# Returning half of a split weight unit early, with shorter split lead and one fewer reserved unit, in a two-layer decoder kernel

## The chip, the cores and the metric

The kernel runs on one core of a Trainium2 chip. The metric is the device time of one execution in microseconds (us), from repeated runs; the profile is of one further execution. Engines are named as in the profile: PE (TensorE matmul) and PEld (its weight load), DVE (VectorE), ACT (ScalarE), POOL (GpSimd), SP (SyncE, which issues nearly all DMAs). A "q" behind a name (SPq, DVEq, PEldq) means the engine's sequencer: branches, waits and DMA issues that don't count as busy.

## The reference, cut to what matters

Two post-norm layers over 256 positions of width 1024. Each has a mixer (chunked gMLP and gated linear attention) and an FFN: dense SwiGLU in layer 0, a top-2-of-8 mixture of SwiGLU experts in layer 1. The mixture is where the time goes:

```python
def swiglu(x, w_gate, w_up, w_down):
    return (jax.nn.silu(x @ w_gate) * (x @ w_up)) @ w_down

def moe_swiglu(x, w_router, e_gate, e_up, e_down):
    ...
    for e in range(N_EXPERTS):
        out = out + gates[:, e:e + 1] * swiglu(t, e_gate[e], e_up[e], e_down[e])
    return out.reshape(B, S, D)
```

The expert width is 3584, so each of the eight experts has three matrices of 1024 x 3584 float32, 14 MB each. All of them are read once from HBM. Of the 256 positions about a quarter go to each expert.

## The kernel before, in words

**Slots and units.** All weights pass through one pool of slots of 128 x 2048 float32 (1 MB each): 16, and 18 once the second mixer has closed. A unit is 1 MB of a weight matrix. `Stream.load` (line 163) takes a slot, `r`, and issues the unit's DMA on SP (L169). `converting` (line 176) takes two more slots, `h` and `l`, and splits the unit into two rounded halves (`split`, line 262: ACT copies `r` to `h` in L263, DVE writes `l = r - h` in L264); then `r` is given back. A unit marked `whole` (the first of each gate product) isn't split: it stays in `r` and PE reads it as plain float32 (L1042). The list `idle` holds free slots: slots are taken from its front and given back at its end, in the order in which the program is written. The wait for the slot's last reader is put on the engine that writes it next.

**Who sets the order.** The program is emitted by hand. A "tick" is one k-step of a product: one tick per 512-column matmul group of a unit, four per unit. At each tick `pump` (line 198) decides what is emitted:

```python
while self.loaded < len(self.plan) and (
        len(idle) > 1 + max(0, self.freed + self.reserve - self.split)):
    self.load()
if not most or self.split >= min(self.cap, len(self.plan)) or len(idle) < 2:
    break
if self.plan[self.split][4] > self.now + lead:
    break
self.convert()
```

So units are split when they are due within `lead` ticks (`LEAD_E = 14` in the mixture, line 36), and loads leave enough idle slots for `reserve` split units that PE hasn't finished with (`NC = 6`, line 34); both are set at line 1185. `free` (line 218) gives back all slots of a unit, and is called for two units at once, behind the second one (L1055 in `product`, L1137 in `down`).

**Experts.** Each expert has four groups of hidden columns, 512, 1024, 1024, 1024 wide (the last expert in reverse order). A group is a gate product, an up product (`product`, line 1027), and then the down product (`down`, line 1112) of the group before, so that the activation (`gated`, `finish`, `transposed`) lies beside matmuls. Before its first group an expert gathers its positions with a one-hot matmul (`gather`, line 1000: `oh` on DVE, L971 to L978, transposed and multiplied on PE, L1004 and L992, then split on ACT and DVE, L983 and L984); after its last group it scatters its result (`scatter`, line 1141: `yh` and `yl` by ACT and DVE, L1154 and L1155 on PE, L1157 on DVE).

**Two ways by a bit.** An expert with at most 64 positions packs the high and low halves of its input side by side, so that a matmul by `h` and one by `l` do the work of three passes; one with more takes three passes. `cases` (line 956) chooses on the chip, with `tc.If(self.wide > 0)` (L961), on PE, ACT and DVE. `wide` is the expression `mask & 2 ** e` (line 900) over a loaded register. In this data six experts take the first way and two (the first and the third) the second. Within a product the second unit's last matmul and the passes that only the three-pass way has stand inside the branch, behind both units (`last_passes`, line 1020); a first unit's `l` is read by matmuls outside the branch alone.

**The end.** `gb` (the last norm's weights) takes a slot at line 1229. A branch for the case that an expert has more than 128 positions follows (L1237, not taken here; its body takes and returns slots of its own while it is emitted). Behind it `y` and `sq` take a slot each (lines 1283 and 1284), and the last norm writes them (`centre`, L1291 on ACT, L1293 on DVE).

Of the kernel before, what the change touches and what calls it, by code (L numbers as in the profile page):

```python
# [8 lines left out]
F32 = mybir.dt.float32  # L9
# [8 lines left out]
D = 1024  # L18
# [12 lines left out]
NX = 2  # L31
NR = 6
NQ = 3
NC = 6
HALF = 64
LEAD_E = 14


@with_exitstack
def trunk(ctx: ExitStack, tc: tile.TileContext, x, w_in, gm_ws, gm_bs, gm_ln_g, gm_ln_b, gla_wa2, gla_ba,  # L40
          gla_norm_g, w_out, ln_mix_g, ln_mix_b, ffn_g, ffn_u, ffn_d, router_w, exp_g, exp_u, exp_d,
          ln_ffn_g, ln_ffn_b, out):
    nc = tc.nc
# [14 lines left out]
    def s2(name, dt=F32, shape=(P, 512)):  # L58
        return act.tile(list(shape), dt, tag="s2", name=name, bufs=6)
# [64 lines left out]
    idle = list(range(NS))  # L124
    room = [wt] * NS

    class Stream:
# [84 lines left out]
        def get(self, key):  # L212
            i = self.index[key]
            while self.split <= i:
                self.convert()
            return self.parts[i]

        def free(self, key):
            assert self.index[key] == self.freed, (key, self.index[key], self.freed)
# [4 lines left out]
    W = Stream()  # L224
# [594 lines left out]
    def moe(xT, ready, consts):  # L819
# [38 lines left out]
        def routing():  # L858
            yield 2
            logits(0)  # L860
            yield 8
            ready.finish()
            logits(1)
            yield 2
            for tb in range(2):
                nc.tensor.matmul(plt[:, tb, :], lTs[tb], pair, start=True, stop=True)
            nc.vector.tensor_copy(lg, plt)
            m1, oh1 = first_max(lg, "1")
            lg2 = const.tile([P, 2, NE], F32, name="lg2")
            nc.vector.scalar_tensor_tensor(lg2, oh1, -3.0e38, lg, op0=ALU.mult, op1=ALU.add)  # L870
            m2, oh2 = first_max(lg2, "2")
            nc.vector.tensor_tensor(sel, oh1, oh2, op=ALU.add)
            W.pump(1, 100)
            ut = s2("ut")[:, 0:P]
            nc.gpsimd.memset(ut, 1.0)
            nc.gpsimd.affine_select(ut, ut, pattern=[[1, P]], compare_op=ALU.is_ge, fill=0.0, base=-1,
                                    channel_multiplier=-1)
            yield 6

            pr = psy("pr", (P, 2, NE))  # L880
            nc.tensor.matmul(pr[:, 0, :], ut, sel[:, 0, :], start=True, stop=True)
            nc.tensor.matmul(pr[:, 1, :], ut, sel[:, 1, :], start=True, stop=False)
            nc.tensor.matmul(pr[:, 1, :], ones, sel[:, 0, :], start=False, stop=True)
            pc = psy("pc", (P, NE))
            for tb in range(2):
                nc.tensor.matmul(pc, ones, sel[:, tb, :], start=tb == 0, stop=tb == 1)
            nc.vector.scalar_tensor_tensor(rk, pr, 1.0, sel, op0=ALU.add, op1=ALU.mult)
            nc.vector.tensor_scalar(rk, rk, -1.0, None, op0=ALU.add)
            nc.vector.tensor_scalar(small, pc, HALF + 0.5, float(-HALF), op0=ALU.is_lt, op1=ALU.mult)

            bits = const.tile([P, NE], F32, name="bits")
            msum = const.tile([P, 1], F32, name="msum")
            nc.vector.scalar_tensor_tensor(bits, pc, HALF + 0.5, powers, op0=ALU.is_gt, op1=ALU.mult)
            nc.vector.tensor_reduce(msum, bits, axis=AX.X, op=ALU.add)
            nc.vector.tensor_copy(mask_i, msum)
            experts[0].one_hot()
            mask = nc.values_load(mask_i[0:1, 0:1], engines=[ET.PE, ET.Activation, ET.DVE], min_val=0,
                                  max_val=2 ** NE - 1)
            for e in range(NE):
                experts[e].wide = mask & 2 ** e  # L900
            W.pump(1, 100)
            yield 1
            yield from experts[0].gather()

            cnt = const.tile([P, 1], F32, name="cnt")
            nc.vector.tensor_reduce(cnt, pc, axis=AX.X, op=ALU.max)
            nc.vector.tensor_copy(cnt_i, cnt)
            W.hold = False
            yield 60

            w12 = const.tile([P, 2, 2], F32, name="w12")
            dl = const.tile([P, 2], F32, name="dl")
            nc.vector.tensor_tensor(dl, m2[:, :, 0], m1[:, :, 0], op=ALU.subtract)
            nc.gpsimd.tensor_tensor(dl, ecst, dl, op=ALU.pow)
            nc.vector.tensor_scalar(w12[:, 0, :], dl, 1.0, None, op0=ALU.add)
            nc.vector.reciprocal(w12[:, 0, :], w12[:, 0, :])
            nc.vector.tensor_tensor(w12[:, 1, :], dl, w12[:, 0, :], op=ALU.mult)
            for tb in range(2):
                nc.vector.tensor_scalar(gates[:, tb, :], oh1[:, tb, :], w12[:, 0, tb:tb + 1], None, op0=ALU.mult)
                nc.vector.scalar_tensor_tensor(gates[:, tb, :], oh2[:, tb, :], w12[:, 1, tb:tb + 1], gates[:, tb, :],  # L920
                                               op0=ALU.mult, op1=ALU.add)
                nc.vector.tensor_scalar(acc[tb], xf[tb], ALPHA, None, op0=ALU.mult)
# [20 lines left out]
        class Expert:  # L943
# [83 lines left out]
            def product(self, units, n, nm):  # L1027

                xh, xl = self.x
                nb = n // 512  # L1030
                p = [psw(f"{nm}{b}") for b in range(nb)]
                kk = 2048 // n
                held, rest, last = [], [], []
                for u, ((wh, wl), free) in enumerate(units):
                    held.append(free)
                    for j in range(kk):
                        k = kk * u + j
                        for b in range(nb):
                            s = slice(b * 512, b * 512 + 512)
                            tick()  # L1040
                            if wl is None:
                                nc.tensor.matmul(p[b], self.xw[:, k, :], wh[:, j, s], start=k == 0, stop=False,  # L1042
                                                 skip_group_check=True)
                                continue
                            nc.tensor.matmul(p[b], xh[:, k, :], wh[:, j, s], start=k == 0, stop=False,  # L1045
                                             skip_group_check=True)
                            rest.append((p[b], xl[:, k, :], wh[:, j, s], False))
                            second = p[b], xh[:, k, :], wl[:, j, s], k == KT - 1
                            if k == KT - 1 or (u % 2, j, b) == (1, kk - 1, nb - 1):
                                last.append(second)  # L1050
                            else:
                                nc.tensor.matmul(*second[0:3], start=False, stop=False, skip_group_check=True)  # L1052
                    if u % 2 and (nb > 1 or u == 1):
                        self.last_passes(rest, last)
                        for free in held:  # L1055
                            free()
                        held, rest, last = [], [], []
                return p
# [53 lines left out]
            def down(self, g, units, first, final):  # L1112
                if first:
                    self.y = ybanks
                held, rest, last = [], ([], []), []
                for u, ((wh, wl), free) in enumerate(units):
                    held.append(free)
                    ch, cl = self.hT[g][u // 2]
                    ending = final and u == 2 * len(self.hT[g]) - 1
                    for n in range(4):  # L1120
# [3 lines left out]
                        y = self.y[hf]  # L1124
# [8 lines left out]
                        else:  # L1133
                            nc.tensor.matmul(y, ch[:, k, :], wl[:, j, s], start=False, stop=False,  # L1134
                                             skip_group_check=True)
                    if u % 2:
                        for free in held:  # L1137
                            free()
                        held, rest = [], ([], [])
# [20 lines left out]

        def stream(keys):
            for key in keys:
                yield W.get(key), lambda key=key: W.free(key)

        experts = [Expert(str(e), lambda tb, e=e: rk[:, tb, e:e + 1], lambda tb, e=e: gates[:, tb, e:e + 1],
                          small[:, e:e + 1]) for e in range(NE)]
# [16 lines left out]
        while W.hold:  # L1183
            tasks["route"].step()
        W.lead, W.reserve = LEAD_E, NC
        for i, t in enumerate((ybanks, ybanks, tbanks, tbanks)):
# [16 lines left out]
        for e, ex in enumerate(experts):  # L1203
            for g, (c0, n) in enumerate(groups(e)):
# [21 lines left out]
                hidden_tasks[e, g] = task  # L1226
                if g == NG - 2 and e + 1 < NE:
                    tasks["gather", e + 1] = Task(experts[e + 1].gather_from_scratch())
        gb, _ = W.slot("gb", F32, 2, D)
        for i, v in enumerate((ln_ffn_g[1], ln_ffn_b[1])):  # L1230
            nc.sync.dma_start(gb[:, i, :], bcast(v, D))
        hidden_tasks[prev].finish()
# [4 lines left out]
        with tc.If(most > P):  # L1237
# [4 lines left out]
            with tc.For_i(0, NE) as ei:  # L1242
# [14 lines left out]
                def units(plan):  # L1257

                    own = Stream()
                    plan(own)  # L1260
                    for key in list(own.index):
                        yield own.get(key), lambda key=key: own.free(key)

                def cols_of(t, g):
                    return units(lambda o: o.cols((), w(t), g * 512, 512))
# [14 lines left out]
                                        op=ALU.add)  # L1280


        y, _ = W.slot("y", F32, 2, D)
        sq, _ = W.slot("sq", F32, 2, D)
        mean, var, ssq = tiny("mean", 2), tiny("var", 2), tiny("ssq", 4).rearrange("p (t h) -> p t h", t=2)
        nc.vector.tensor_tensor(mean, total[:, :, 0], total[:, :, 1], op=ALU.add)
        nc.vector.tensor_scalar(mean, mean, -1.0 / D, None, op0=ALU.mult)
# [103 lines left out]
```

## Time and profile before

| | |
|---|---|
| three runs | 1353.36, 1355.66, 1359.66 us (median 1355.66) |
| profiled execution, own time | 1355.74 us |
| its span, first to last instruction | 1354.0 us |
| mean granted TensorE clock | 0.984 |
| busy: PE, DVE, ACT | 1297.6 (96%), 1067.0 (79%), 842.3 us (62%) |
| read from HBM | 423.86 MB, 314 GB/s over the span |
| the mixture | from about 421 us to 1342 us |

Busy PE is an upper bound, since matmuls overlap in the pipeline and their ends are modelled. In a table of stretches each row gives a stretch's bounds and length, then per engine busy time and (instructions), then the granted TensorE clock, the mean busy share of the 16 DMA engines and the bandwidth. The share is that of transfers that start in the stretch, so a stretch can read slightly over 1. In a table of waits a row is "engine line <- releaser: total, times, longest". In a timeline a row is start, duration, engine, line, operation, and in brackets the idle time before.

### The profile page before, as it was taken

The page shows a single profiled execution, that of the slowest core. Times are in us where ns is not written, and L with a number is a line of the kernel's source. Part 1 is how long each engine was busy: PE and PEld are TensorE (multiplying, and loading weights), DVE is VectorE, ACT ScalarE, POOL GpSimd, SP SyncE. Part 2 cuts the span into 40 slices and gives each one's busy share as a digit, 9 for nine tenths or more (in the row PEclk, how much of TensorE's full clock was granted, in tenths as well). Part 3 has the DMA queues.
Part 4 walks back from the last instruction along what each step waited for, and adds up shares of the span by engine and source line. Part 5 has one row for each costly group of instructions (what it writes and reads, how often), then busy time and mean ns, then how long its engine had stood idle before and what let it go on. Part 6 is the DMA issues. An engine that isn't in the chain of part 4 may idle for free. (4 is left out here: it accounts for less than half of the span.)

```text
span 1354.0 us, 17754 instructions
## 1 busy us (share of the span) xinstructions
PE 1297.6 (96%) x6113; PEld 1034.9 (76%) x6113; DVE 1067.0 (79%) x965; ACT 842.3 (62%) x702; POOL 38.4 (3%) x79
## 2 busy tenths in 40 slices
PE   9999999999999999999999999989899999998995
PEld 7878888888787787787678778768776776776773
DVE  6687544386684988898977889889799898978987
ACT  5654444336433766676666678768577687767674
POOL 1012000000110000000000000000000000000000
PEclk9999999999999999999999999999899999999897
DMA  9636655444473699999998999999899999999993
GB/s 342 254 132 216 240 189 204 171 156 156 153 291 147 263 357 357 347 411 350 412 391 344 345 345 409 376 412 400 354 383 411 413 380 410 411 354 413 369 409 122
DMA packets 118770, 426.39 MB, mean 315 GB/s; under 512 B 8089, under 2 KB 10722, under 8 KB 104578
## 3 DMA queue, kind: packets, MB, share of 16 engines
q1 hardware_dynamic: 117218, 420.61, 80.3%
q0 software_dynamic: 1440, 4.33, 1.1%
q8 instruction: 65, 1.06, 0.3%
q14 instruction: 47, 0.39, 0.1%
HBM read 423.86 MB, written 1.05 MB: 314 GB/s over the span
## 5 line engine op out<-in xcount | busy, mean ns | idle before, releaser
L264 DVE TENSOR_TENSOR l<-r,h 128x2048 fp32r<-128x2048 f32 (+2 forms) x373 | 832.0, 2249 | 120.0 <-ACT h L263 106.3
L263 ACT ACTIVATE h<-r 128x2048 fp32r<-128x2048 f32 (+2 forms) x373 | 689.3, 1882 | 136.3 <-DVE l L264 31.6
L1127 PE MATMUL bank<-h,che 128*128 128x512 f32 x440 | 174.3, 396 | 0.0
L1045 PE MATMUL eu<-h,exh 128*128 128x512 f32 x440 | 167.4, 389 | 0.0
L1134 PE MATMUL bank<-l,che 128*128 128x512 f32 x377 | 148.3, 393 | 0.8 <-DVE l L264 0.8
L1052 PE MATMUL eu<-l,exh 128*128 128x512 f32 x361 | 140.6, 389 | 0.3 <-DVE l L264 0.3
L1045 PE MATMUL eg<-h,exh 128*128 128x512 f32 x316 | 128.7, 420 | 0.0
L1042 PE MATMUL eg<-r,xw 128*128 128x512 f32 x248 | 120.5, 621 | 0.0
L1127 PEld LDWEIGHTS bank<-h,che 128*128 128x128 f32 x440 | 83.1, 189 | 16.5
L1045 PEld LDWEIGHTS eu<-h,exh 128*128 128x128 f32 x440 | 82.6, 188 | 17.1
L1052 PE MATMUL eg<-l,exh 128*128 128x512 f32 x237 | 92.7, 391 | 0.1
L1134 PEld LDWEIGHTS bank<-l,che 128*128 128x128 f32 x377 | 71.2, 189 | 17.2 <-DVE l L264 3.3
L1052 PEld LDWEIGHTS eu<-l,exh 128*128 128x128 f32 x361 | 67.7, 188 | 14.8 <-DVE l L264 0.7
L1042 PEld LDWEIGHTS eg<-r,xw 128*128 128x128 f32 x248 | 47.3, 199 | 41.4 <-issue 39.4
L1045 PEld LDWEIGHTS eg<-h,exh 128*128 128x128 f32 x316 | 59.8, 189 | 16.3 <-issue 4.9
L258 PE MATMUL f<-h,xhm 128*128 128x512 f32 (+1 forms) x192 | 72.2, 376 | 0.0
L259 PE MATMUL f<-l,xhm 128*128 128x512 f32 (+1 forms) x192 | 71.4, 372 | 0.0
L260 PE MATMUL f<-h,xlm 128*128 128x512 f32 (+1 forms) x192 | 71.4, 372 | 0.0
L1098 PEld LDWEIGHTS bank<-fold,sge 128*128 128x128 f32 x336 | 45.0, 196 | 13.3 <-DVEq L961 7.3
L1052 PEld LDWEIGHTS eg<-l,exh 128*128 128x128 f32 x237 | 44.6, 188 | 13.0 <-issue 3.0
L1098 PE MATMUL bank<-fold,sge 128*128 128x64 f32 x336 | 45.0, 277 | 4.8 <-DVEq L961 4.8
L1098 PE MATMUL bank<-fold,upe 128*128 128x64 f32 x336 | 47.1, 284 | 0.0
(354 smaller groups left out, 1770.3 us busy)
## 6 DMA issues: line engine op xcount, KB each, us to landing
r<-in_exp_w_gate SPq DMA_DIRECT2D x112, 1024.0 KB, 8.9
r<-in_exp_w_up SPq DMA_DIRECT2D x112, 1024.0 KB, 9.5
r<-in_exp_w_down SPq DMA_DIRECT2D x110, 1024.0 KB, 12.6
r<-in_w_in SPq DMA_DIRECT2D x17, 1024.0 KB, 8.6
r<-in_ffn_w_gate SPq DMA_DIRECT2D x11, 1024.0 KB, 6.8
r<-in_ffn_w_up SPq DMA_DIRECT2D x11, 1024.0 KB, 5.2
r<-in_ffn_w_down SPq DMA_DIRECT2D x11, 1024.0 KB, 4.9
r<-in_w_out SPq DMA_DIRECT2D x8, 1024.0 KB, 9.3
```

Of the source, the lines that this page charges most:

```text
L258: nc.tensor.matmul(ps, xh, wh, start=start, stop=False)
L259: nc.tensor.matmul(ps, xh, wl, start=False, stop=False)
L260: nc.tensor.matmul(ps, xl, wh, start=False, stop=stop)
L263: nc.scalar.activation(dst_h, src, AF.Copy)
L264: nc.vector.tensor_tensor(dst_l, src, dst_h.bitcast(F32), op=ALU.subtract)
L1042: nc.tensor.matmul(p[b], self.xw[:, k, :], wh[:, j, s], start=k == 0, stop=False, skip_group_check=True)
L1045: nc.tensor.matmul(p[b], xh[:, k, :], wh[:, j, s], start=k == 0, stop=False, skip_group_check=True)
L1052: nc.tensor.matmul(*second[0:3], start=False, stop=False, skip_group_check=True)
L1098: nc.tensor.matmul(tp[:, j, i * HALF:i * HALF + HALF], hidden_columns(t, j), fold, start=True, stop=True)
L1127: nc.tensor.matmul(y, ch[:, k, :], wh[:, j, s], start=first and u + j == 0, stop=False, skip_group_check=True)
L1134: nc.tensor.matmul(y, ch[:, k, :], wl[:, j, s], start=False, stop=False, skip_group_check=True)
```

## The change

The change has four parts. `drop` gives back the slot of `l` of a first unit (even place in its pair) as soon as that unit's matmuls are emitted, in `product` and in `down`; the slot of `h` stays until the pair is done. `LEAD_E` goes from 14 to 12 ticks and `NC` from 6 to 5 units. The bit of each expert is put into a register once, by `nc.snap`, instead of standing as an expression in each branch. And `y` and `sq` take their slots together with `gb`, ahead of the last down product and of the branch L1237.

```diff
-NC = 6
+NC = 5
 HALF = 64
-LEAD_E = 14
+LEAD_E = 12
...
+        def drop(self, key):
+
+            i = self.index[key]
+            if i not in self.whole:
+                sh, sl = self.held[i]
+                self.held[i] = sh,
+                idle.append(sl)
...
-                experts[e].wide = mask & 2 ** e
+                experts[e].wide = nc.snap(mask & 2 ** e)
...
-                for u, ((wh, wl), free) in enumerate(units):
+                for u, ((wh, wl), free, drop) in enumerate(units):
...
+                    if u % 2 == 0:
+                        drop()
                     if u % 2 and (nb > 1 or u == 1):
                         self.last_passes(rest, last)
                         for free in held:
...
-                    if u % 2:
+                    if u % 2 == 0:
+                        drop()
+                    else:
                         for free in held:
                             free()
                         held, rest = [], ([], [])
...
-                yield W.get(key), lambda key=key: W.free(key)
+                yield W.get(key), lambda key=key: W.free(key), lambda key=key: W.drop(key)
...
-        gb, _ = W.slot("gb", F32, 2, D)
+        gb, y, sq = [W.slot(nm, F32, 2, D)[0] for nm in ("gb", "y", "sq")]
...
-        y, _ = W.slot("y", F32, 2, D)
-        sq, _ = W.slot("sq", F32, 2, D)
```

## Rows read from the trace of the kernel before

**Rows 1.** Stretches: a two-pass expert, a three-pass expert, most of the two-pass experts
```profile
core 0: us, PE busy (x) PEld busy (x) DVE busy (x) ACT busy (x) POOL busy (x), PEclk, DMA share, GB/s
554.90:664.60 109.70, 106.13 (x491) 83.13 (x490) 98.07 (x72) 81.10 (x63) 0.00 (x0) 0.98 0.96 379
664.60:793.00 128.40, 125.88 (x559) 99.22 (x558) 102.71 (x69) 81.87 (x61) 0.00 (x0) 1.00 0.93 364
...
820.00:1320.00 500.00, 471.79 (x2204) 370.63 (x2204) 440.95 (x326) 366.13 (x289) 0.00 (x0) 0.98 0.99 393
```

**Rows 2.** Stretches of one two-pass expert: quiet, gather, short group, scatter
```profile
1040.70:1071.70 31.00, 31.00 (x161) 25.39 (x160) 28.70 (x19) 24.16 (x19) 0.00 (x0) 1.00 1.02 411
1071.70:1106.90 35.20, 31.96 (x165) 25.49 (x164) 29.92 (x29) 24.79 (x22) 0.00 (x0) 1.00 0.98 383
1106.90:1125.00 18.10, 18.10 (x83) 13.95 (x81) 16.19 (x11) 13.44 (x11) 0.00 (x0) 1.00 1.02 411
1015.10:1040.70 25.60, 22.25 (x89) 16.27 (x88) 24.15 (x19) 19.44 (x16) 0.00 (x0) 1.00 1.02 412
```

**Rows 3.** Stretches: the other gather groups of two-pass experts
```profile
847.20:881.50 34.30, 31.89 (x164) 25.42 (x164) 29.07 (x26) 24.47 (x21) 0.00 (x0) 1.00 0.97 376
957.90:996.90 39.00, 34.20 (x164) 27.27 (x164) 31.57 (x29) 26.28 (x22) 0.00 (x0) 0.91 0.87 339
...
1182.20:1218.60 36.40, 33.54 (x164) 26.73 (x164) 29.50 (x27) 24.41 (x21) 0.00 (x0) 0.95 0.93 358
```

**Rows 4.** Timeline of SP's load issues at a gather; SP's longest wait, 820 to 1320
```profile
957.04 6.67 SPq L169 DMA_DIRECT2D r<-in_exp_w_down  x4
977.42 0.38 SPq L169 DMA_DIRECT2D r<-in_exp_w_gate  x1
...
SPq L169 <- DVE l L264: 307.1, 67, 13.6
```

**Rows 5.** Stretches: scatter groups behind the three-pass expert and behind two-pass ones
```profile
793.00:816.20 23.20, 22.00 (x89) 16.37 (x88) 21.42 (x15) 18.17 (x14) 0.00 (x0) 1.00 0.91 347
902.40:926.80 24.40, 21.64 (x84) 16.64 (x85) 22.89 (x16) 18.11 (x14) 0.00 (x0) 0.93 1.02 397
...
1125.00:1151.20 26.20, 23.75 (x90) 16.98 (x89) 24.36 (x19) 19.93 (x16) 0.00 (x0) 0.93 1.02 410
1247.30:1284.40 37.10, 32.49 (x138) 24.43 (x138) 33.86 (x28) 25.90 (x20) 0.00 (x0) 0.91 0.96 372
```

**Rows 6.** PE's waits, 820 to 1320
```profile
PE bank L1155 <- DVE yl L264: 9.9, 4, 2.7
PE bank L1004 <- DVE oh L978: 7.8, 4, 3.6
...
PE bank L1134 <- DVE l L264: 0.2, 1, 0.2
```

**Rows 7.** Groups by line, 820 to 1320: the two halves of a split
```profile
line engine op names shapes xcount | busy us, mean ns | idle before us <-releasers
L264 DVE TENSOR_TENSOR l<-r,h 128x2048 fp32r<-128x2048 f32 x171 | 387.8, 2289 | 36.8 <-ACT h L263 30.8 <-DVEq L961 1.6
L263 ACT ACTIVATE h<-r 128x2048 fp32r<-128x2048 f32 x170 | 319.2, 1916 | 60.5 <-DMA r<-in_exp_w_gate 25.5 <-PE eg L1042 9.6 <-DMA r<-in_exp_w_up 7.2
```

**Rows 8.** PE's timeline inside a down product
```profile
947.02 0.39 PE L1134 MATMUL bank<-l,che 128*128 128x512 f32 x1
947.24 0.39 PE L1127 MATMUL bank<-h,che 128*128 128x512 f32 x1
```

**Rows 9.** Line L961, the branch on an expert's bit; who waited for it
```profile
L961 DVEq ALU_OP  x308: 40/40/57, 415.7 to 1331.7; - x154
...
  PEld bank L1098: 7.3, 12
  PE bank L1098: 4.8, 7
```

**Rows 10.** The end: PE's branch at L1237, ACT's wait at L1291, DVE's timeline
```profile
L1237 PEldq COMPARE_BRANCH  x1: 3447/3447/3447, 1340.3 to 1340.3; - x1
...
L1291 ACTq EVENT_SEMAPHORE  x1: 1450/1450/1450, 1342.5 to 1342.5; - x1
...
1344.00 2.08 DVE L1293 SCALAR_TENSOR_TENSOR y<-acc,mean,gb 128x512 f32<-128x512 f32 x3 [1.53 <-PEq L1237]
```

More of the change, by code (lines that the diff above doesn't have):

```diff
@@ L1115, in down @@
                 held, rest, last = [], ([], []), []
-                for u, ((wh, wl), free) in enumerate(units):
+                for u, ((wh, wl), free, drop) in enumerate(units):
                     held.append(free)
@@ L1261, in units @@
                     for key in list(own.index):
-                        yield own.get(key), lambda key=key: own.free(key)
+                        yield own.get(key), lambda key=key: own.free(key), lambda key=key: own.drop(key)
                 def cols_of(t, g):
```

## The prediction

> **What bounds the kernel now.** I read the page's engine shares and slices first: PE is 96% busy over the span, so the question is what the remaining idle is worth, and where. The change touches the mixture alone, so next come stretches of that stage. A two-pass expert took 109.7 us, the whole of 820 to 1320 moved 393 GB/s with PE busy for 471.79 of 500 us, and the three-pass expert kept PE busy for 125.88 of 128.4 us [rows 1]. So both PE and the loads are nearly full, and neither alone is the bound.
>
> The next view cuts one two-pass expert into its four groups [rows 2]. In the quiet group PE never idles (31.00 of 31.00 us) and DMA is full too, at 411 GB/s. A unit of 1,048,576 bytes at 411 GB/s takes 2.55 us, and the group's 12 units 30.6 us: PE and DMA tie. In the gather group PE idles 3.2 us and DMA falls to 383 GB/s. In the scatter group PE idles 3.3 of 25.6 us while DMA is full: there the loads bound. So the loss moves in a circle: at the gather the store of loaded units is full and DMA stops; a group later the store is empty and PE waits for what DMA didn't bring.
>
> The timeline shows the stop: SP issued its last load at about 963.7 and the next at 977.4 [rows 4], since a load waits for the slot that a split gives back (307.1 us of SP's waits end with DVE's L264, same rows) and the splits stood behind the gather's work on ACT and DVE. What is lost by gather, against 411 GB/s: (411 - 383) / 411 x 35.2 = 2.4 us [rows 2], and by the same sum 2.9, 6.8 and 4.7 us [rows 3]. Together 16.8 us in four experts.
>
> **The change, part by part.** *Room.* The planner loads while more than 1 + (NC - S) slots are idle, S being the split units that PE still holds. With 18 slots and two per split unit, the loaded, unsplit units are at most 18 - 2S - 1 - (NC - S), that is 11 - S with NC = 6 and 12 - S with NC = 5: one more at the same S. An early-returned `l` is one slot for half of a pair's time, less the whole units: 0.4 on average, which goes to loads as well. The lead of 12 alone shifts units from split to unsplit and adds nothing to their sum. So 1.4 units more are on hand, 1.4 x 2.55 = 3.6 us of DMA time that a gather can outlast before DMA stops. Of the four losses it covers 2.4, 2.9, 3.6 and 3.6: 12.5 us. What can PE make of them? The scatter group tells: behind the three-pass expert, where the store was full, it took 23.2 us; behind two-pass experts 24.4 and 26.2 [rows 5], and 25.6 in rows 2. Down to 23.2 that is 1.2 + 3.0 + 2.4 = 6.6 us; the last expert's wider scatter group (37.1 us with PE busy for 32.49, rows 5) may give some 3. That makes 9.6 us at most and nothing at least, if the quiet groups, already full on PE, can't use it. I take two thirds, 6.5, nearer the scatter of 23.2 us, because that row is this kernel with a full store. The two-pass expert ahead of the three-pass one (109.7 us) gives at most 109.7 - 42 x 2.55 = 2.6; I take 1.
>
> On the page's rule: the loads ran at 411 GB/s with PE full [rows 2], and I use that as their ceiling. The Trainium skill, "DMA: Bandwidth & Descriptors", section "Where 436 GB/s comes from", says that for HBM to SBUF the HBM side binds at about 358 GB/s per core; by it no load could be brought sooner and this term would be 0. The trace disagrees (393 GB/s over 500 us, rows 1), so the measurement decides.
>
> *Clock.* PE's clock was granted at 0.91 and 0.95 of full in the gathers at 957.9 and 1182.2, against 1.00 in those at 847.2 and 1071.7; PE's busy time there is 34.20 and 33.54 against 31.89 and 31.96 us [rows 2, 3]. So the two longer stops also cost 2.3 and 1.6 us at the lower level (1.2 GHz), after PE had idled. All or none of these 3.9 us return; I take 2, half.
>
> *Lead and slots.* A matmul pass starts 0.22 to 0.23 us after the last [rows 8], two per k-step: two k-steps less lead place a split 4 x 0.227 = 0.9 us later in PE's order. DVE's small work at a gather and a scatter then stands behind fewer splits: PE waited 9.9 us in 4 scatters for `yl` and 7.8 us in 4 gathers for `oh` [rows 6]. Gain 0 to 8 x 0.9 = 7.3; I take 1, since the split that no longer stands ahead is missed later. Against it: following the list of idle slots, a split of an odd unit k takes slots of the pair that ends with unit k - 4 (k - 6 before). From there to its use PE has 3 units x 8 x 0.227 = 5.4 us, and the split needs 1.92 + 2.29 = 4.2 us [rows 7]. That fits by 1.2 us, but PE takes 1.8 us per unit and DVE 2.29, so the third unit in a row has none left. Now PE waits 0.2 us in all for `l` in these 500 us [rows 6], so the cushion exists today; the loss is between 0 and 0.9 us in each of 24 groups (four per two-pass expert, six such experts), 22 us. I take 2, nearer to the row that shows almost no waits.
>
> *Moved loads.* Loads are emitted earlier, and one waits on PE (a dropped `l`) where it waited on a split before. SP issues in order, so a later load stands behind it; but PE's event lies a whole store ahead of the data's use, and each load's issue is short against 2.55 us. I cost this at nothing; the cover is the depth of the store, and without it a load would be late by up to one unit, 2.6 us.
>
> *Bits.* DVE's sequencer runs 308 register operations of 40 ns in L961 [rows 9], ACT and PE about as many: 12.3 us of sequencer time each at most, 8 of them put back once. They lie under instructions of up to 2.3 us, apart from chains where an engine waits for a branch: 12 and 7 waits on PEld and PE [rows 9], 19 x 0.04 = 0.8 us. I take 0.8, between 0 and 12.3, as most branches stand under running splits.
>
> *Last slots.* Behind L1237 `y` and `sq` have slots that the branch's body had, so ACT and DVE wait for PE to pass it: PE's branch took 3.447 us, ACT's wait 1.45 and DVE's 1.53 us [rows 10]. With slots from ahead their last users are long done: 1.4 us, on the path that ends the kernel. What is late next is the mean on DVE, ready when the wait began. Between 0, if the wait comes from elsewhere, and 1.5.
>
> **The sum.** 6.5 + 1 + 2 + 1 - 2 + 0.8 + 1.4 = 10.7 us less. The profiled execution took 1355.74 us (span 1354.0), like the median of 1355.66, so it stands for it: 1355.7 - 10.7 = 1345.0.
>
> **The rivals.** *A: the loads are full already.* Quiet groups show PE and DMA at their ends together, and what a deeper store saves at the gather is spent waiting on the same DVE and ACT work. Only bits and end remain: 1355.7 - 2.2 = 1353.5. For it: in the quiet and the short group PE has no idle time at all [rows 2]. Against it: the 23.2 us scatter group. The case that the change doesn't do what it says (SP, in order, keeps its loads no further ahead) gives the same time. The 358 GB/s that the Trainium skill states (same page and section) would lead to this time too; after the 393 GB/s of rows 1 that cause has 0.01 of this rival's chance.
>
> *B: splits arrive late.* One mechanism: with slots only from the pair four units back, PE catches DVE at the end of each run of split units and waits the 0.9 us by which the split moved. In 24 groups that is 21.8 us; with half of the loads' gain (3.8) and 2.2 for bits and end it ends 15.8 us slower, 1371.5. It decides from 0.5 us a group on, where 24 x 0.5 = 12 eats the other terms. For it: DVE is busy for 28.70 of 31.00 us in the quiet group [rows 2]. Against it: 0.2 us of such waits now.
>
> *C: everything recoverable returns*: 9.6 + 2.6 + 3.9 + 2.2 = 18.3 us, and some of the 17.7 us for `yl` and `oh`: 4 more makes 1333.
>
> **How the numbers follow.** Forecast and C together 0.55 (C 0.1 of it), A 0.30, B 0.15. About 0.5%, 6.8 us, is what a measurement of this kernel can tell from no change. Of the forecast's own 0.45 some 0.05 falls short of it, so faster is 0.50. Same: A's 0.30, that 0.05, less 0.01 of A beyond the bound, 0.34. Slower: B and that 0.01, 0.16. The range takes in C (1333.0) and A, and reaches toward B as far as a mild form of it, 0.6 us in each of 24 groups (14.4), with 3.8 and 2.2 back and 2 less on clocks: 1362.0. Beyond lie the heavy part of B, about 0.1, and as much below 1333. The forecast's own range is 1337 to 1350.
>
> **What would show it.** Right: the gather groups at 39.0 and 36.4 us nearer 35 with DMA above 390 GB/s; scatter groups at 23 to 24 us; SP's gap of 13.7 us at the gather shorter; clock in those stretches at 1.00; ACT's wait at L1291 gone and the end after the last scatter 1.4 us shorter; no register operations in L961. Wrong: PE's waits for DVE's L264 (`l`) well above 0.2 us between 820 and 1320, in the up and down products, with DMA no fuller than before (B); or gather and scatter groups as they are with the store deeper (A). If the loss were not the store's depth but the chain of `oh`, `exh` and the splits behind it, the gathers would keep their length, and the forecast would fall with its largest term.

## The result, and the profile after

The changed kernel takes **1342.82 us** (median of six runs, 1341.95 to 1343.10) against 1358.51 us for the kernel before in the same series: a ratio of 0.9893, interval [0.9876, 0.9909]. The profiled execution took 1342.48 us, with a span of 1340.8 against 1354.0 and a mean granted clock of 0.996 against 0.984. The lines behind L218 have moved by some 8 to 12: the split is L271 (ACT) and L272 (DVE), the branch on a bit L969, the gather's `oh` L979 to L986, the scatter's matmuls L1166 and L1167, its addition L1169.

The stretches of the mixture, cut at the first plain-float32 matmul of a group's gate product:

```profile
core 0: us, PE busy (x) PEld busy (x) DVE busy (x) ACT busy (x) POOL busy (x), PEclk, DMA share, GB/s
554.90:664.30 109.40, 106.21 (x490) 81.49 (x489) 98.08 (x73) 78.63 (x63) 0.00 (x0) 1.00 0.98 388
...
961.60:994.80 33.20, 32.15 (x164) 25.35 (x164) 29.08 (x26) 24.40 (x21) 0.00 (x0) 1.00 1.01 392
1038.50:1071.10 32.60, 31.97 (x161) 25.19 (x160) 30.41 (x20) 23.41 (x19) 0.00 (x0) 1.00 1.01 409
1071.10:1104.30 33.20, 32.19 (x165) 25.38 (x164) 29.11 (x26) 24.39 (x21) 0.00 (x0) 1.00 1.01 394
...
1180.20:1213.40 33.20, 32.16 (x165) 25.38 (x164) 29.09 (x26) 24.39 (x21) 0.00 (x0) 1.00 1.00 390
796.10:820.00 23.90, 22.60 (x90) 16.25 (x89) 21.22 (x14) 18.88 (x14) 0.00 (x0) 1.00 0.91 350
...
1122.40:1147.60 25.20, 22.87 (x89) 16.14 (x89) 23.70 (x18) 18.85 (x14) 0.00 (x0) 1.00 1.02 407
1241.80:1274.20 32.40, 30.65 (x138) 22.82 (x138) 30.75 (x24) 22.99 (x17) 0.00 (x0) 1.00 1.02 411
...
820.00:1320.00 500.00, 483.74 (x2262) 371.66 (x2261) 457.11 (x335) 377.38 (x301) 0.00 (x0) 1.00 1.00 400
```

Read against [rows 1, 2, 3, 5]: every gather group of these takes 33.20 us, where it took 34.3, 39.0, 35.2 and 36.4, and the clock is at its upper level (2.4 GHz) in all of them. The scatter groups behind two-pass experts take 25.2 us, the last expert's 32.4 instead of 37.1. The quiet group, which had no idle time on PE, is longer: 32.60 against 31.00 us, with PE busy for 31.97. Over 820 to 1320 the loads moved 400 GB/s instead of 393.

Added up over the span, from the starts of the groups in both traces (minus is time saved). The first row ends where the first expert's third group starts (459.4 and 463.2); the runs below are measured from there too:

| stretch | before, us | after, us | difference |
|---|---|---|---|
| up to the first expert's third group | 459.4 | 463.2 | +3.8 |
| from there to the three-pass expert's scatter | 333.6 | 332.9 | -0.7 |
| 4 quiet groups | 124.1 | 130.2 | +6.1 |
| 4 gather groups | 144.9 | 132.8 | -12.1 |
| scatter groups, 4 and the last expert's | 139.2 | 131.9 | -7.3 |
| short groups and the last expert's other two | 110.4 | 111.7 | +1.3 |
| last group's start to the end | 42.4 | 38.1 | -4.3 |
| span | 1354.0 | 1340.8 | -13.2 |

The waits show where it comes from. In the kernel before, between 820 and 1320, ACT's split waited for loads, and PE at the gather for `oh` [rows 6]:

```profile
ACT h L263 <- DMA r<-in_exp_w_gate: 25.5, 25, 3.6
...
ACT h L263 <- PE eg L1042: 9.6, 3, 5.1
...
ACT h L263 <- DMA r<-in_exp_w_up: 7.2, 11, 1.4
ACT h L263 <- DMA r<-in_exp_w_down: 6.4, 6, 2.8
...
ACT h L263 <- PE eg L1024: 5.0, 4, 2.1
```

After, in the same stretch, no row shows ACT's split waiting for a DMA, and of the wait for `oh` 0.8 us are left, on PE's weight load. What ACT's split and PE wait for now:

```profile
ACT h L271 <- PE bank L1032: 9.4, 13, 0.8
ACT h L271 <- PE eg L1032: 7.9, 4, 2.1
ACT h L271 <- PE eg L1050: 7.2, 4, 1.8
PE bank L1167 <- DVE yl L272: 4.1, 3, 1.4
PE bank L1166 <- DVE acc L1169: 3.0, 4, 0.9
```

So ACT's split, which waited 25.5 + 7.2 + 6.4 = 39.1 us for data, waits for none. For PE, which still reads the slots that the split will write, it waits 9.4 + 7.9 + 7.2 = 24.5 us; it waited 16.6 us for PE before (9.6 + 5.0, and 2.0 in two smaller rows), so most of the 39.1 us is gone and not merely moved. PE's wait for `yl` fell from 9.9 us [rows 6] to 4.1.

The gather at 957.88 in the kernel before shows what a late split did to `oh`:

```profile
960.43 1.91 ACT L263 ACTIVATE h<-r 128x2048 fp32r<-128x2048 f32 x1 [0.38 <-DMA r<-in_exp_w_up]
...
960.60 2.29 DVE L264 TENSOR_TENSOR l<-r,h 128x2048 fp32r<-128x2048 f32 x1
962.80 0.48 DVE L971 TENSOR_SCALAR oh<-iota,rk 128x128 f32<-128x128 f32 x2
...
964.26 0.66 PE L1004 MATMUL bank<-ident,oh 128*128 128x128 f32 x2 [3.59 <-DVE oh L978]
```

and the same gather after, whose group starts at 961.64:

```profile
956.80 4.67 DVE L272 TENSOR_TENSOR l<-r,h 128x2048 fp32r<-128x2048 f32 x2
...
962.50 0.48 DVE L979 TENSOR_SCALAR oh<-iota,rk 128x128 f32<-128x128 f32 x2
...
964.27 0.38 PE L1012 MATMUL bank<-ident,oh 128*128 128x128 f32 x2
```

Before, the split ahead of `oh` had waited for its load and ended on DVE 5.0 us after the group's start, and PE stood still for 3.59 us. After, it ends 0.2 us before the start, and PE doesn't wait.

Two things got worse. PE's weight load of `l` in the down product waits for DVE more often; before, 820 to 1300, it was 1.8 us in 5 waits, and after

```profile
PEld bank L1144 <- DVE l L272: 12.8, 25, 0.7
```

And the routing, where the eight registers are filled. PE's timeline:

```profile
417.25 0.47 PE L266 MATMUL e<-h,xhm 128*128 128x512 f32 x1 [3.13 <-issue]
```

and the groups of line L908 on PE's queue (count, shortest/median/longest ns, first and last start):

```profile
L908 PEldq ALU_OP  x8: 32/32/42, 415.8 to 417.0; - x8
L908 PEldq MOVE  x8: 29/29/37, 415.9 to 417.2; - x8
```

PE stood still for 3.13 us where it had stood for 1.61: the 16 register operations run from 415.8 to 417.2, about 0.09 us apart, on an engine that has nothing else queued.

At the end, ACT's wait for the branch is gone [rows 10]. What ends its idle time now is DVE's mean, and `y` follows the mean by 0.2 us:

```profile
1330.89 0.72 ACT L1301 ACTIVATE sq<-acc,mean 128x512 f32<-128x512 f32 x1 [4.32 <-DVE mean L1297]
...
1330.63 0.17 DVE L1297 TENSOR_SCALAR mean<-mean 128x2 f32<-128x2 f32 x1
1330.83 2.08 DVE L1303 SCALAR_TENSOR_TENSOR y<-acc,mean,gb 128x512 f32<-128x512 f32 x3
```

### The profile page after: what moved, and what is told of

Same layout as the page of the kernel before. It is cut to its first block, busy times and chain, and to the rows that moved or that the text cites. A ratio compares the mean times of both kernels' runs of the same rounds, so it can differ in the third digit from the quotient of the medians.

```text
span 1340.8 us, 16964 instructions
## 1 busy us (share of the span) xinstructions
PE 1296.5 (97%) x6113; PEld 1024.0 (76%) x6113; DVE 1068.5 (80%) x965; ACT 839.0 (63%) x702; POOL 37.7 (3%) x79
## 5 line engine op out<-in xcount | busy, mean ns | idle before, releaser
L272 DVE TENSOR_TENSOR l<-r,h 128x2048 fp32r<-128x2048 f32 (+2 forms) x373 | 833.3, 2249 | 134.0 <-ACT h L271 117.6
L271 ACT ACTIVATE h<-r 128x2048 fp32r<-128x2048 f32 (+2 forms) x373 | 685.0, 1881 | 124.1 <-PE bank L1032 39.1
L1144 PE MATMUL bank<-l,che 128*128 128x512 f32 x377 | 153.3, 407 | 7.0 <-DVEq L969 3.5
L1050 PE MATMUL eg<-r,xw 128*128 128x512 f32 x248 | 114.5, 595 | 0.0
L1050 PEld LDWEIGHTS eg<-r,xw 128*128 128x128 f32 x248 | 45.2, 190 | 39.6 <-issue 37.8
L1110 ACT ACTIVATE hide<-bank 128x256 f32<-128x256 f32 x42 | 16.1, 384 | 71.7 <-PE bank L1108 71.7
L1075 ACT ACTIVATE sge<-eg 128x512 f32<-128x512 f32 x55 | 30.2, 595 | 36.4 <-PE eg L1032 36.3
## 6 DMA issues: line engine op xcount, KB each, us to landing
r<-in_exp_w_down SPq DMA_DIRECT2D x110, 1024.0 KB, 11.6
```

What stands on the lines that cost most here:

```text
L271: nc.scalar.activation(dst_h, src, AF.Copy)
L272: nc.vector.tensor_tensor(dst_l, src, dst_h.bitcast(F32), op=ALU.subtract)
L1075: nc.scalar.activation(o, i, f)
```

## The experiments

The theories, in words: **depth** (the prediction's: more units on hand at the gather, so loads don't stop), **lead** (fewer splits stand ahead of the gather's and scatter's small work), **order** (which slot a split or a load gets, and so what it must wait for), with the registers and the last slots as terms of their own. In the expectations, theory 1 is depth, 2 lead, 3 the bits in registers, and 4 and 5 are forms of order. Twelve kernels ran in three series (1 to 4, 5 to 8, 9 to 12); medians of the kernel before in these were 1359.86, 1359.6 and 1356.92 us, and ratios are each to its own series.

**1. Early return and last parts alone, room 6 and lead 14 as before.**

```diff
 (after)
-NC = 5
+NC = 6
-LEAD_E = 12
+LEAD_E = 14
```

> The changed kernel with room for six split units and a lead of 14 again; the early return, the registers and the last slots stay. Theory 1 (depth of the store, paid for by later splits): the store is about 0.9 unit (2.4 us) shallower, so the gather groups, 33.2 us in the changed kernel, lengthen by 1 to 2.5 us each; the quiet groups go from 32.6 back to 31.0 us since splits get older slots. Net 3 to 8 us slower than the changed kernel's 1342.8: 1346 to 1351. Theory 2 (the lead alone: fewer splits ahead of the gather's work on DVE): PE's wait for oh, gone in the changed kernel, is back with 1 to 3.6 us per gather. Theory 3 (the bits are the gain, 300 register operations fewer per engine): no difference over 2 us.

Measured: 1490.14 us, ratio 1.0956 [1.0935, 1.0977], which no theory expected. The two largest waits of ACT and DVE, 820 to 1300:

```profile
ACT h L271 <- DVE l L272: 132.5, 48, 5.5
DVE l L272 <- ACT h L271: 98.4, 73, 2.0
```

and the same 480 us as a stretch:

```profile
820.00:1300.00 480.00, 418.92 (x1799) 317.75 (x1797) 364.63 (x264) 301.04 (x237) 0.00 (x0) 0.94 0.88 339
```

ACT waits for DVE and DVE for ACT, and loads fall to 339 GB/s. Following the list of idle slots in the program gives the reason: one slot given back early turns the list by a place, and 59 of 171 splits then write `h` into the slot that the split just ahead still reads as `r`, so two engines that used to overlap take turns. Run 10 puts that to the test.

**2. The changed kernel with the old lead.**

```diff
 (after)
-LEAD_E = 12
+LEAD_E = 14
```

> The changed kernel with the lead alone back at 14 steps. Theory 1: the sum of loaded and split units on hand stays at 11.4, splits take the same slots of the pair four units back, so the time stays within 3 us of 1342.8 and the quiet groups at 32.6 us. Theory 2: the wait for oh at the gathers is back (1 to 3.6 us each, five or six of them), 5 to 12 us slower. Theory 3: no difference.

Measured: 1371.92 us, 1.0088 [1.0074, 1.0102]: 29 us above the changed kernel, which no theory expected either. The gather keeps its 33.2 us without the new lead, so the lead isn't what cured `oh`. A scatter group took 28.9 us (1030.6 to 1059.5), 3.7 more than with lead 12, and PE waits 12.5 us for the scatter's addition, where it waits 3.0 in the changed kernel (820 to 1300):

```profile
PE bank L1166 <- DVE acc L1169: 12.5, 4, 3.3
```

Run 6 shows the same without the other edits.

**3. No early return.**

```diff
 (after)
         def drop(self, key):
...
             i = self.index[key]
-            if i not in self.whole:
...
-                idle.append(sl)
+            return
```

> The changed kernel without the early return of a first unit's second part. Theory 1: 0.4 unit fewer on hand, 1.0 us of cover per gather: 2 to 5 us slower, seen in gather and scatter groups; quiet groups unchanged. Theories 2 and 3: within 2 us of 1342.8.

Measured: 1342.12 us, 0.9870 [0.9855, 0.9886], against 1342.82 for the changed kernel. The early return is worth nothing here. ACT's split waits 15.8 us for PE in this run (820 to 1320, three rows added), less than the changed kernel's 24.5 and no more than the 16.6 before, so that sum is no measure of the gain; waits for loads there are none.

**4. The bits as expressions again.**

```diff
 (after)
-                experts[e].wide = nc.snap(mask & 2 ** e)
+                experts[e].wide = mask & 2 ** e
```

> The changed kernel with the bits as expressions in each branch again, not in registers. Theory 1: PE's idle time at the routing, 3.1 us in the changed kernel, falls back to 1.6 us and the half clock after it goes, about 3 us gained there; 300 register operations per engine return under running work and cost about 1: 1340 to 1342. Theory 3: 5 to 12 us slower, up to the whole gain.

Measured: 1340.9 us, 0.9861 [0.9845, 0.9878], 1.9 us below the changed kernel by the medians. The intervals of the two overlap, so the traces decide. PE's stop at the routing is the old one:

```profile
415.64 0.49 PE L266 MATMUL e<-h,xhm 128*128 128x512 f32 x1 [1.61 <-DVE slot L984]
```

From the first expert's third group to the end both kernels take the same (1339.2 - 461.6 and 1340.8 - 463.2, both 877.6 us). So the register operations at the branches cost nothing, and filling registers cost 1.5 us at the routing.

**5. Lead 12 alone.**

```diff
 (before)
-LEAD_E = 14
+LEAD_E = 12
```

> The kernel before with the lead alone at 12 (room for six, no early return, bits and last slots as before). Followed through the list of idle slots, splits take slots of the pair five or six units back, as before. Theory 1 (store depth: the unit that room for five adds): the sum on hand stays at 10.0 units, so gathers and scatters stay as before: within 4 us of the kernel before (ratio 0.997 to 1.003), quiet groups at 31.0 us. Theory 2 (the lead: fewer splits ahead of DVE's work for gather and scatter): most of the gain, 10 us or more, ratio 0.988 to 0.993, PE's wait for oh gone, and with quiet groups at 31.0 us perhaps below the changed kernel.

Measured: 1359.27 us, 0.9997 [0.9978, 1.0016]. Nothing, and PE's wait for `oh` stays (820 to 1300):

```profile
PE bank L1004 <- DVE oh L978: 8.8, 4, 3.4
```

**6. Room for five alone.**

```diff
 (before)
-NC = 6
+NC = 5
```

> The kernel before with room for five alone (lead 14, no early return). Theory 1 as it stood before the last runs: 11.0 units on hand, about 8 us faster than before. Theory 4, formed on the run with the lead back at 14 (room for five makes a split wait for the pair four units back, and with a lead of 14 that split stands ahead of the scatter's work on DVE and ACT, which PE waits for): as slow as that run, ratio 1.005 to 1.015, scatter groups near 24.7 us and PE waiting 3 us in each for acc.

Measured: 1368.05 us, 1.0060 [1.0043, 1.0076]: slower (the profiled execution took 1372.32, the longest of its twelve). An expert's quiet, gather, short and scatter group:

```profile
945.50:978.00 32.50, 31.91 (x161) 25.12 (x160) 30.33 (x20) 23.23 (x19) 0.00 (x0) 1.00 1.01 405
978.00:1011.20 33.20, 32.18 (x164) 25.38 (x164) 29.20 (x26) 24.18 (x21) 0.00 (x0) 1.00 1.00 390
1011.20:1029.40 18.20, 18.20 (x83) 13.95 (x83) 16.39 (x13) 15.07 (x12) 0.00 (x0) 1.00 1.02 409
1029.40:1058.70 29.30, 24.48 (x90) 17.25 (x89) 24.02 (x18) 18.88 (x14) 0.00 (x0) 0.94 0.94 362
```

and waits, 820 to 1300:

```profile
ACT h L263 <- PE eg L1024: 24.4, 4, 6.8
...
PE bank L1154 <- DVE acc L1157: 12.5, 4, 3.3
```

This is the run that takes the result apart. Room for five by itself brings both the shorter gather (33.20) and the longer quiet group (32.50), and pays at the scatter, 29.3 us. There ACT's split waits up to 6.8 us for PE, DVE's half of it waits behind, and the scatter's addition (`acc`) that PE needs next is late. Run 2 has the same 12.5 us; with two k-steps less lead than run 2 and nothing else changed (that is the changed kernel) PE waits 3.0 us for `acc`, and the scatter group falls to 25.2.

**7. `y` and `sq` behind the branch again.**

```diff
 (after)
-        gb, y, sq = [W.slot(nm, F32, 2, D)[0] for nm in ("gb", "y", "sq")]
+        gb, _ = W.slot("gb", F32, 2, D)
...
+        y, _ = W.slot("y", F32, 2, D)
+        sq, _ = W.slot("sq", F32, 2, D)
```

> The changed kernel with y and sq taken behind the branch again. All theories: ACT and DVE wait again for PE to pass the branch, 1.4 us slower than 1342.8, all of it behind the last scatter. If it is within 0.5 us, the wait at the end came from elsewhere.

Measured: 1343.95 us, 0.9880 [0.9850, 0.9911], by the medians 1.1 us above the changed kernel's 1342.82. The intervals of the two overlap, so the trace decides: the old wait is back at the end.

```profile
DVE y L1305 <- PEq L1249: 1.4, 1, 1.4
```

**8. The registers filled twenty steps later**, the first expert keeping its expression.

```diff
 (after)
-            for e in range(NE):
-                experts[e].wide = nc.snap(mask & 2 ** e)
+            experts[0].wide = mask & 1
...
-            yield 60
+            yield 20
+            for e in range(1, NE):
+                experts[e].wide = nc.snap(mask & 2 ** e)
+            yield 40
```

> The changed kernel with seven of the eight registers filled 20 steps later, inside expert 0's work (expert 0 keeps the expression). If the registers cost time only because PE's queue is empty at the routing (PE idle 3.1 us there against 1.6 without them, then half clock), the time is that of the kernel without registers, 1340.9, give or take 1. If the registers cost time by themselves, it stays at 1342.8.

Measured: 1340.1 us, 0.9850 [0.9820, 0.9881]. The seven fills now run behind queued matmuls, and PE's stop at the routing is 1.61 us again, and from the first expert's third group to the end it takes 1337.1 - 459.8 = 877.3 us, so nothing is lost later. So it was the empty queue that made them dear, not their number.

**9. One slot less.** No early return, and 17 slots instead of 18.

```diff
 (after, drop returns at once)
-            idle.extend(range(NS, NS + NX))
+            idle.extend(range(NS, NS + NX - 1))
```

> The changed kernel without the early return (1342.1) and with one of the 18 slots left unused: followed through the planner, splits take the same slots as in the changed kernel, and the units on hand fall from 11.0 to 10.0, as many as in the kernel before. Theory 1 (the gain is the depth that room for five gives): gathers and scatters starve as before, 7 to 16 us slower than 1342.1. Theory 5 (the gain is the order: with a lead of 12 and slots of the pair four units back, ACT and DVE cannot run ahead into the gather's and scatter's way, whatever the depth): within 3 us of 1342.1, gather groups at 33.2 and no wait for oh.

Measured: 1342.65 us, 0.9886 [0.9865, 0.9906]: the whole gain is still there. By the prediction's own formula this kernel has 17 - 2S - 1 - (5 - S) = 11 - S unsplit units on hand, what the kernel before had. A gather group:

```profile
1072.10:1105.30 33.20, 32.14 (x165) 25.38 (x164) 29.11 (x26) 24.29 (x21) 0.00 (x0) 1.00 1.01 397
```

and the larger of ACT's waits for loads (820 to 1300):

```profile
ACT h L268 <- DMA r<-in_exp_w_gate: 5.2, 7, 1.3
```

That ends the theory of depth as the prediction counted it, in units on hand. SP still pauses at this gather: the timeline of its load issues has

```profile
1067.81 4.96 SPq L169 DMA_DIRECT2D r<-in_exp_w_down  x3
1083.45 5.29 SPq L169 DMA_DIRECT2D r<-in_exp_w_gate  x2
```

with 10.7 us between, as in the changed kernel (962.3 to 973.0), and yet DMA stays nearly full. The pause is 3 us shorter than the 13.7 of [rows 4], with no more units on hand than there. A pause of 11.6 us (1075.8 to 1087.4) went with 383 GB/s at a gather before [rows 2], where this one goes with 397. So the pause that the prediction started from isn't by itself the loss. The Trainium skill, "Perfetto Trace Analysis", section "Optimization Strategy", says that consistent bubbles can mean too little SBUF for the next tile. Here a megabyte less brought no bubble back.

**10. Room 6 and lead 14 with another choice of slots.** As run 1, but in the mixture a load takes first a slot that a split gave back, and a split first one that PE gave back.

```diff
 (after, NC = 6, LEAD_E = 14)
+    raws, by_kind = set(), []
...
-            n = idle.pop(0)
+            n = next((i for i in idle if (i in raws) == raw), idle[0]) if by_kind else idle[0]
+            idle.remove(n)
+            raws.discard(n)
...
+            raws.add(slot)
...
+        by_kind.append(True)
```

> The early return with room for six and a lead of 14, which took 1490 us, with one thing changed: in the mixture loads take slots that a split gave back (a raw unit's) first, splits take slots that PE gave back first. If the 1490 us came from the list alone (the early return turns the list by one place, so that 59 of 171 splits write their first part into the slot that the split just ahead reads, and ACT and DVE take turns), that goes: splits take slots of pairs five or six units back again, ACT's wait for L264 falls below 10 us, and the time is near the kernel before or some us below it (10.4 units on hand against 10.0): 1346 to 1358. If it came from something else in the early return, it stays over 1400.

Measured: 1346.12 us, 0.9915 [0.9894, 0.9936]. From 1490.14 by nothing but which free slot is taken: run 1's cost was the order of the list. `oh` is late as before (7.4 us in 4 waits, 820 to 1300), and ACT waits 19.6 us for gate loads.

**11. The same with lead 12, and the registers late.**

```diff
 (run 10)
-LEAD_E = 14
+LEAD_E = 12
...
```

> The same with a lead of 12 and seven registers filled late. Theory 1: 10.4 units on hand, 0.4 more than before, and quiet groups at 31.0 us: 1340 to 1352. Theory 5: no gain without the slots of four units back: 1352 to 1358.

Measured: 1339.14 us, 0.9866 [0.9844, 0.9889]. An expert's four groups:

```profile
1028.30:1059.20 30.90, 30.90 (x162) 25.48 (x160) 27.48 (x18) 23.67 (x19) 0.00 (x0) 1.00 1.02 413
1059.20:1097.60 38.40, 33.70 (x165) 27.09 (x164) 31.07 (x29) 25.93 (x22) 0.00 (x0) 0.96 0.96 375
1097.60:1115.70 18.10, 18.10 (x82) 13.93 (x81) 17.41 (x13) 14.22 (x11) 0.00 (x0) 1.00 1.02 408
1115.70:1139.00 23.30, 21.95 (x90) 16.49 (x89) 22.09 (x16) 17.73 (x15) 0.00 (x0) 1.00 1.02 411
```

and PE's wait at the gather (820 to 1300):

```profile
PE bank L1018 <- DVE oh L992: 9.7, 4, 3.8
```

A second way to about the same time, with the profile of the kernel before: a quiet group without idle time (30.90), a long gather (38.40) with its wait for `oh`, a short scatter (23.30). These four take 110.7 us, the same four took 110.5 in the kernel before (1040.7 to 1151.2) and 109.1 in the changed kernel (1038.5 to 1147.6), so this expert alone shows no gain. Cut as in the table above, the run gains at the scatter groups (129.7 us against 139.2), at the end (38.2 against 42.4) and ahead of the three-pass expert's scatter (329.8 against 333.6), while its gathers cost more than before (147.4 against 144.9). The expectation from order is missed: it had no gain without the slots of four units back. So neither those slots nor the cure of `oh` is needed for this time. Runs 8 and 11 are below the changed kernel by median, but the intervals of all three overlap, so none is shown the better.

**12. Lead 10**, no early return, registers late.

```diff
 (after, drop returns at once)
-LEAD_E = 12
+LEAD_E = 10
...
```

> The changed kernel without the early return, with a lead of 10 and seven registers filled late. Theory 1 (11.0 units on hand, as with 12): gathers and scatters as in the changed kernel, but splits stand two steps later: PE's waits for L264's l grow, quiet groups 32.6 to 34 us; 1340 to 1352. Theory 5: as much or more is gained at gather and scatter as fewer splits stand ahead of them: 1335 to 1341.

Measured: 1349.17 us, 0.9936 [0.9915, 0.9957], 7 us above run 3 by the medians. Order's expectation (1335 to 1341) is missed, and depth's (1340 to 1352) is met, as it also counted on late splits. Less lead makes splits late elsewhere: PE's weight loads of `l` in the up product wait 6.5 us, against 0.9 us in 4 waits in the changed kernel (820 to 1300):

```profile
PEld eu L1059 <- DVE l L269: 6.5, 16, 0.7
```

and a gather group, at 33.20 us in the changed kernel, takes 34.40:

```profile
1073.80:1108.20 34.40, 32.77 (x164) 25.07 (x164) 29.04 (x26) 24.28 (x21) 0.00 (x0) 1.00 0.97 379
```

## Why the prediction was right, and where it was wrong

The time (1345.0 against 1342.82) and the sign were right; by the ratios it said 0.8% less, and 1.07% was measured. That the total came so near is in part luck, since large misses offset each other. For gathers and scatters the loads, the clock and the lead had 6.5 + 2 + 1 = 9.5 us, and 19.4 were saved; quiet and short groups cost 6.1 + 1.3 us where 2 stood for later splits, and the stretch up to the first expert's third group cost 3.8 us, for which the sum had no term. The largest term was right in sign, but neither in size nor in reason.

Of the signs that it named, the gathers (33.2 us at 390 to 396 GB/s), SP's shorter pause, the clock and the end came. The scatter groups of 23 to 24 us did not (25.2), and one sign against it came too: waits for `l` in the down product, though with DMA fuller than before.

**Loads and the store's depth (-6.5, at most 9.6): the step that failed.** The prediction counted 1.4 units more on hand, 1.0 from the room and 0.4 from the early return. Without the 0.4 (run 3) and with 1.0 fewer (run 9) the time stays within 0.7 us. The trace paid for gathers and scatters 12.1 + 7.3 = 19.4 us, twice the "at most", though the clock's part below is in it. What the runs show in its place is what the splits wait for, and which small work stands behind them. With room for five, splits wait for loads no more (39.1 us before, none in runs 3 and 6, 5.2 + 0.8 = 6.0 in run 9); at the gather no late split stands ahead of `oh`, and PE's 7.8 us there [rows 6] are gone. The scatter's part comes only when the lead falls as well (run 2 against the changed kernel). The prediction saw this chain, but as what would prove it wrong: it said that then "the gathers would keep their length". The chain was right and this consequence wrong, because the edit to the room cut the chain.

**Lead (-1, at most 7.3): mis-sized, because it was costed by itself.** Alone it is worth nothing (run 5); room alone costs 8.5 us (run 6: 1368.05 against 1359.6); together they save 17.7 (run 3: 1342.12 against 1359.86, registers and last slots nearly even in it). On top of room for five the lead alone is worth 28.4 us in the profiled spans (run 2's 1369.2 against 1340.8) and 29.1 by the medians. A sum of parts, each judged in the kernel before, cannot give that: the split that stands ahead of the scatter's addition does harm only when it must wait for PE's slots.

**Later splits (+2, at most 22): the right kind, too small.** Slots from the pair four units back make PE catch DVE, as rival B had it, and in a place it named (waits for `l` in the down product): quiet groups take 32.5 us with room for five alone (run 6) and 30.9 with room for six in run 11. The size was 1.5 to 1.6 us in each quiet group, 6.1 in four, near 0.4 us for each of an expert's four groups, just below the 0.5 from which B would have decided.

**Clock (-2, half of 3.9): right in kind, and nearly all of it came.** In the two gathers that ran at 0.91 and 0.95 [rows 3], PE's busy time fell from 34.20 and 33.54 to 32.15 and 32.16 us at a clock of 1.00, 3.4 us. That about 2 are left in the total is luck, as the rest went where the prediction didn't look, at the routing: from PE's restart there to the first expert's third group it took 44.3 us before and 46.0 after. The same 46.0 stands in run 4, which fills no registers, and the dip (0.92 from 405 to 427 in both) also in runs 5 and 6, which change one constant each, but not in run 8 (1.00). So it isn't shown to be the change's doing.

**The expert before the three-pass one (-1)**: 109.7 to 109.4, so 0.3. **Moved loads (0)**: right by run 3.

**Bits (-0.8): wrong in sign.** The branches' operations were hidden altogether (run 4), so nothing came back; the prediction counted the fills as "8 of them put back once" and never asked where they stand. They stand where PE has drained, for +1.5.

**Last slots (-1.4): right**, 1.1 us by run 7's median and 1.4 by its trace; the late one next is DVE's mean, as forecast. The other 2.8 us of the end's 4.3 came with room for five in run 6, which takes 39.6 us for that stretch without the new slots (1331.0 to 1370.6), where the kernel before took 42.4; but run 11 gets to 38.2 with room for six, so room isn't the only way there.

One row was read short. Of the scatter groups behind two-pass experts the one given as 24.4 us began at 899.7, not 902.4, and took 27.1 [rows 5]: the loss at scatters was 2.7 us larger than the sum had it.

On the loads' ceiling the trace goes on differing from the 358 GB/s of the Trainium skill ("DMA: Bandwidth & Descriptors", "Where 436 GB/s comes from"): it shows 400 GB/s over 500 us and 411 in the last scatter group.

**What stays open.** Why loads stay full in run 9 with as few units on hand as before was argued from the list of slots (where a load takes a slot that a split gave back, that split stands 5 to 8 k-steps earlier there, and 3 before), and no run varied that distance alone. Followed in the same way, the changed kernel takes most such slots 1 k-step after the split, and its loads are full too, so the distance in k-steps can't be the whole reason. Counted in units, that split lies 7 to 9 back in run 9, 8 to 10 in the changed kernel, and 6 or 7 before: a depth of that kind, which the prediction's formula doesn't count, isn't ruled out. Run 10 shows that the choice of slot matters; it doesn't show which of these is the cause in run 9. Run 11 reaches the same time with splits that wait 20.1 + 8.0 + 3.7 = 31.8 us for loads (820 to 1300), so the account above holds for the changed kernel and not for every way to this time; why that run gains wasn't followed further.

## What to carry to other kernels

When buffers are taken from one list in program order, a constant like the room or the lead also decides whose last read each writer waits for: follow the list for some rounds before costing such an edit, and expect two constants to act together. A wait on data and a wait on a consumer's slot look alike on the engine, but what queues behind them differs, so ask at each small latency-bound step which large instruction stands ahead of it and what that one waits for. Fill registers where the engine has work queued.

## What the runs showed of the hardware that was not expected

Sixteen register operations of 29 to 42 ns each on PE's queue took 1.4 us, some 0.09 us apiece, and held PE for 1.5 us; with matmuls queued ahead (run 8) fourteen of them cost nothing that the trace shows (877.3 us behind them against 877.6). And the order in which equal buffers are reused, with room, lead and the number of slots the same, was worth 144 us of 1490 (runs 1 and 10).
